# First chunks of the up projection through other banks and buffers, and the output projection queued one block later

## The chip, the cores and the metric

One core of a Trainium2 chip runs the whole program. The metric is the device time of one execution in microseconds (us), as the median of several runs. The engines are named as the profile names them: PE (matmuls and transposes), ACT (activations and copies), DVE (elementwise operations and scans), POOL, and SP, which here issues nearly all DMAs.

## The reference

One step of a decoder layer, in float32, for a prompt of 2048 tokens with 16 meta tokens ahead of it and for 8 decode sequences of one token each. What matters here, for the prompt:

```python
h = rmsnorm(xp, norm_mix_g)
q, k, v, u = project_mix(h, w_in)                 # 8 heads of 64, and 512 pooling channels
o_attn = stick_breaking(q, k, v, ...)             # blocks of 128 queries
o_pool = multiscale_pool(u, ...)
xp = xp + concat([o_attn, o_pool]) @ w_out        # 1024 x 1024
h2 = rmsnorm(xp, norm_ffn_g)
up = h2 @ w_up                                    # 1024 x 5632, causal conv of width 3, gate
xp = xp + (silu(gate) * val) @ w_down             # 2816 x 1024
y_prompt = rmsnorm(xp, norm_final_g)
```

`stick_breaking` gives each earlier key the weight sigmoid(z) times the product of (1 - sigmoid(z)) over the keys between it and the query. The decode tokens go through the same layer with cached keys and values of 4096 positions, read through a page table.

## The kernel before

All large matmuls are done in three passes (`mm3`, lines 156 to 161): both operands are split into a high and a low part (`split`, lines 152 to 154: a copy on ACT, then a subtraction on DVE), and high x high, high x low and low x high are added up in one PSUM bank.

The stages follow each other in the program text. Instructions are not issued in that order: a planner, run when the program is built, walks all instructions with estimated times and gives each engine its own fixed queue. Among instructions that it holds ready it takes the one that stands first in the text. On the chip each engine then works through its queue in order and waits on semaphores. So moving a call in the text changes its rank and with it the queues.

*Attention* (`attention`, lines 383 to 529) goes through four pairs of heads. For a pair, the units are a block `bi` of 128 queries (-1 is the meta tokens, then 0 to 15) by a chunk `c` of up to 512 keys. `chain` makes the scores `z` (line 450), two sigmoids on ACT, a scan along the keys on DVE (line 458) and a product on POOL or DVE (line 463). `weigh` follows three units later (LAG): transposes (line 493), copies, and products with the values into the bank `po` (line 508). After a block's last unit, `po` is copied to `ot`, stored to the DRAM tensor `cat_s` (line 517), and `done(bi)` is called.

For the last pair of heads `done` is `out_tile` (lines 573 to 593), the output projection of 128 rows. It loads those rows of `cat_s` into `cr` (line 578), splits them into `ch` and `cl`, does 48 matmuls into two `pso` banks (pool `ps_mm`), adds the residual (line 588), stores `xp_s`, normalises (`rstd_of`, line 592) and stores to `h2_s` (line 593). Row tile 1 + bi of `h2_s` is written by `out_tile(bi)`.

*Up projection* (lines 638 to 885). The 2048 rows are four chunks of 512 (`h2c[0]` to `h2c[3]`), held transposed and split, 32 KB per partition each. Iteration `it` takes the weights of one pair of 128-column slices (gate and value), and the two chunks of a half; each group is 24 matmuls into a `psu` bank. Ahead of the loop the first two chunks are made:

- Chunk 0 (lines 640 to 650): four loads of 128 rows (`xn0`, which shares the three `uwr` slots of the weights' pool `pu_w`), and for each load two groups of four transposes into a bank of `pu_mm` (six banks), each followed by `split`.
- The first weights, `load_up(0)` and `load_up(NF)` (line 671), through the same `uwr` slots.
- Chunk 1 by `h2_chunk(1)` (lines 655 to 669): two loads of 256 rows into slots of the decode's pool (`kvd`), and eight groups of transposes through the only bank of `pu_t`.

After that come the decode's preparations: `state_conv` through `kvd` slots and `pu_t` (lines 674 to 688), eight small loads of the page table `pt4` (lines 694 to 696), the index arithmetic on DVE (lines 699 to 703), and gathers of keys and values that run between the up projection's iterations.

Memory. The left pool of the attention stage (`pb`) and the right pool of the output projection (`pc`: its weights and rows) are closed before the up projection; the new pools lie over their bytes and banks, and a new tile waits for the old tiles that it covers (`reuse_waits="tile"`). The PSUM banks in order of the attention stage are: `ps_mm` 0 and 1, `ps_z` 2 and 3, `ps_t` 4 to 6, `ps_o` 7. The up projection's are `pu_q` 0, `pu_mm` 1 to 6, `pu_t` 7. In SBUF the new pools are stacked from where `pb` began: `pu_w` 36 KB, `h2a` 32 KB (chunk 0), `pu` 12 KB, `h2b` 2 x 32 KB (chunks 1 and 2), then the decode's pool.

Of the kernel before, what the change touches and what calls it, by code (L numbers as in the profile page):

```python
# [8 lines left out]
F32 = mybir.dt.float32  # L9
F32R = mybir.dt.float32r  # L10
# [5 lines left out]
PSUM = bass.MemoryType.PSUM  # L16
DRAM = bass.MemoryType.DRAM

P = 128
D = 1024  # L20
NK = D // P
# [9 lines left out]
NF = DFF // P  # L31
# [6 lines left out]
TILES = [(0, NS + META)] + [(NS + META + P * i, P) for i in range(SEQ // P)]  # L38
# [8 lines left out]
CW = 512  # L47
NCH = SEQ // CW
NSB = NS + 4
NSO = NS + 2  # L50
# [3 lines left out]
def f32(ap):  # L54
    return ap.bitcast(F32)
# [3 lines left out]
def hymba_kernel(  # L59
# [7 lines left out]
    nc = tc.nc  # L67
# [11 lines left out]
    def x_rows(dst, i):  # L79
        if i == 0:  # L80
            nc.sync.dma_start(out=dst[0:NS, :], in_=x_sample)
            nc.sync.dma_start(out=dst[NS:NS + META, :], in_=meta_tokens)
        else:
            return nc.sync.dma_start(out=dst, in_=x_prompt[P * (i - 1):P * i, :])
# [7 lines left out]
    h2_s = dram.tile([ACOLS, D], F32, name="h2_s")  # L92
# [6 lines left out]
    ident = con.tile([P, P], F32, name="ident")  # L99
# [26 lines left out]
    hsm = con.tile([P, NK, 32], F32, name="hsm")  # L126
# [3 lines left out]
    def rstd_of(pool, xt, n, sq=None):  # L130
        ss = pool.tile([P, 1], F32, name="ss")
        if sq is None:
            sq = pool.tile([P, D], BF16, name="sq", bufs=1)
        else:
            sq = pool.tile([P, D], BF16, name="sq", tag=sq[0], bufs=sq[1])
        nc.scalar.activation(out=sq[:n, :], in_=xt[:n, :], func=AF.Square, accum_out=ss[:n, :])
        ms = pool.tile([P, 1], F32, name="ms")
        nc.vector.tensor_scalar(out=ms[:n, :], in0=ss[:n, :], scalar1=1.0 / D, scalar2=EPS, op0=ALU.mult, op1=ALU.add)
        r = pool.tile([P, 1], F32, name="rr")
        t = pool.tile([P, 1], F32, name="rt")  # L140
        ri, ti = r.bitcast(I32), t.bitcast(I32)
        nc.vector.tensor_single_scalar(ti[:n, :], ms[:n, :].bitcast(I32), 1, op=ALU.logical_shift_right)
        nc.vector.tensor_scalar(out=ri[:n, :], in0=ti[:n, :], scalar1=-1.0, scalar2=float(0x5F3759DF),
                                op0=ALU.mult, op1=ALU.add)
        for _ in range(3):
            nc.vector.scalar_tensor_tensor(out=t[:n, :], in0=r[:n, :], scalar=r[:n, 0:1], in1=ms[:n, :],
                                           op0=ALU.mult, op1=ALU.mult)
            nc.vector.tensor_scalar(out=t[:n, :], in0=t[:n, :], scalar1=-0.5, scalar2=1.5, op0=ALU.mult, op1=ALU.add)  # L148
            nc.vector.tensor_tensor(out=r[:n, :], in0=r[:n, :], in1=t[:n, :], op=ALU.mult)
        return r  # L150

    def split(hi, lo, src):
        nc.scalar.copy(hi, src)  # L153
        nc.vector.tensor_tensor(out=lo, in0=src, in1=f32(hi), op=ALU.subtract)  # L154

    def mm3(ps, terms):
        n = len(terms)
        for i, (ah, al, bh, bl) in enumerate(terms):
            nc.tensor.matmul(ps, ah, bh, start=i == 0, stop=False)  # L159
            nc.tensor.matmul(ps, ah, bl, start=False, stop=False)  # L160
            nc.tensor.matmul(ps, al, bh, start=False, stop=i == n - 1)  # L161
# [5 lines left out]
    psm = main.enter_context(tc.tile_pool(name="ps_mm", bufs=2, space=PSUM, reuse_waits="tile"))  # L167
    psz = main.enter_context(tc.tile_pool(name="ps_z", bufs=2, space=PSUM, reuse_waits="tile"))
    pst = main.enter_context(tc.tile_pool(name="ps_t", bufs=3, space=PSUM, reuse_waits="tile"))
# [403 lines left out]
    def out_tile(bi):  # L573
        if bi < 0:
            return
        c0, n = TILES[bi + 1]
        cr = pc.tile([P, NK, P], F32, name="cr")
        nc.sync.dma_start(out=cr, in_=cat_s[:, :, c0:c0 + n].rearrange("c p n -> p c n"))
        ch = pc.tile([P, NK, P], F32R, name="ch", bufs=CHB)
        cl = pc.tile([P, NK, P], F32R, name="cl", bufs=CHB)  # L580
        split(ch, cl, cr)
        xt = pc.tile([P, D], F32, name="xt2", bufs=2)
        x_rows(xt, bi + 1)
        for hf in range(2):
            cs = slice(hf * 512, (hf + 1) * 512)
            ps = psm.tile([P, CW], F32, name="pso", tag="psm")
            mm3(ps, [(ch[:, c, :], cl[:, c, :], wo[c][0][:, cs], wo[c][1][:, cs]) for c in range(NK)])
            nc.vector.tensor_tensor(out=xt[:, cs], in0=ps, in1=xt[:, cs], op=ALU.add)
        nc.sync.dma_start(out=xp_s[c0:c0 + n, :], in_=xt)
        xn = pc.tile([P, D], F32, name="xn2")  # L590
        r = rstd_of(pc, xt, n, sq=("xn2", 1))
        nc.vector.scalar_tensor_tensor(out=xn, in0=xt, scalar=r[:, 0:1], in1=gffn, op0=ALU.mult, op1=ALU.mult)
        nc.sync.dma_start(out=h2_s[c0:c0 + n, :], in_=xn)

    attention(3, [], out_tile)
    main.close()


    puw = ctx.enter_context(tc.tile_pool(name="pu_w", bufs=3, reuse_waits="tile"))
    h2ctx = ctx.enter_context(ExitStack())  # L600
    pha = h2ctx.enter_context(tc.tile_pool(name="h2a", bufs=1, reuse_waits="tile"))
    h2c = {}

    def load_up(f):
        wr = puw.tile([P, NK, P], F32, name="uwr")
        nc.sync.dma_start(out=wr, in_=w_up[:, f * P:(f + 1) * P].rearrange("(c p) f -> p c f", p=P))
        wh = puw.tile([P, NK, P], F32R, name="uwh")
        wl = puw.tile([P, NK, P], F32R, name="uwl")
        split(wh, wl, wr)
        return wh, wl  # L610
# [12 lines left out]


    psq = ctx.enter_context(tc.tile_pool(name="pu_q", bufs=1, space=PSUM, reuse_waits="tile"))
    psm = ctx.enter_context(tc.tile_pool(name="pu_mm", bufs=6, space=PSUM, reuse_waits="tile"))
    pst = ctx.enter_context(tc.tile_pool(name="pu_t", bufs=1, space=PSUM, reuse_waits="tile"))
    HF = NF // 2

    def load_act(pool, hf, a0, n):  # L630
# [5 lines left out]
        return ah, al  # L636

    with ExitStack() as es:
        pu = es.enter_context(tc.tile_pool(name="pu", bufs=2, reuse_waits="tile"))
        h2c[0] = pha.tile([P, 2, NK, CW], F32R, name="h2c")  # L640
        for a in range(4):
            xn = puw.tile([P, NK, P], F32, name="xn0", tag="uwr").rearrange("p c n -> p (c n)")
            nc.sync.dma_start(out=xn, in_=h2_s[TILES[1 + a][0]:TILES[2 + a][0], :])
            for c4 in range(0, NK, 4):
                tp = psm.tile([P, 4, P], F32, name="tp0", tag="psu")
                for c in range(4):
                    nc.tensor.transpose(tp[:, c, :], xn[:, (c4 + c) * P:(c4 + c + 1) * P], ident)
                if a == 0:
                    nc.vector.tensor_copy(hsm[:, c4:c4 + 4, NSO:NSB], tp[:, :, 0:2])
                split(h2c[0][:, 0, c4:c4 + 4, a * P:(a + 1) * P], h2c[0][:, 1, c4:c4 + 4, a * P:(a + 1) * P], tp)  # L650
        phb = es.enter_context(tc.tile_pool(name="h2b", bufs=2, reuse_waits="tile"))
        dec = es.enter_context(ExitStack())
        dp = dec.enter_context(tc.tile_pool(name="dec", bufs=KVB, reuse_waits="tile"))

        def h2_chunk(ch):

            h2c[ch] = (pha if ch == 3 else phb).tile([P, 2, NK, CW], F32R, name="h2c")
            for a2 in range(0, 4, 2):
                c0 = TILES[1 + 4 * ch + a2][0]
                xn2 = dp.tile([P, 4, 512], F32, name="xn3", tag="kvd").rearrange("p k f -> p (k f)")  # L660
                nc.sync.dma_start(out=xn2.rearrange("p (a d) -> p a d", a=2),
                                  in_=h2_s[c0:c0 + 2 * P, :].rearrange("(a p) d -> p a d", p=P))
                for a in (a2, a2 + 1):
                    xn = xn2[:, (a - a2) * D:(a - a2 + 1) * D]
                    for c4 in range(0, NK, 4):
                        tp = pst.tile([P, 4, P], F32, name="tp3")
                        for c in range(4):
                            nc.tensor.transpose(tp[:, c, :], xn[:, (c4 + c) * P:(c4 + c + 1) * P], ident)
                        split(h2c[ch][:, 0, c4:c4 + 4, a * P:(a + 1) * P], h2c[ch][:, 1, c4:c4 + 4, a * P:(a + 1) * P], tp)

        ws_first = [load_up(0), load_up(NF)]
        h2_chunk(1)
        sc_v = state_conv.rearrange("b j f -> (b j) f")
        for f0 in range(0, 44, 11):
            room = dp.tile([P, 4, 512], F32, name="sc", tag="kvd").rearrange("p k f -> p (k f)")
# [18 lines left out]
        for b in range(NB):  # L694
            nc.sync.dma_start(out=pt4[:, b:b + 1],
                              in_=page_table[b, :].rearrange("(n o) -> n o", o=1).unsqueeze(1).broadcast_to([NPAGE, 4, 1]))
# [375 lines left out]
```

## Time and profile before

| | |
|---|---|
| median of 3 runs | 2898.42 us (2897.55 to 2900.72) |
| the profiled execution | 2897.86 us, its span 2895.9 us |
| PE busy | 2735.5 us, 94% of the span |
| DVE busy | 1822.0 us, 63% |
| ACT busy, POOL busy | 1040.0 us, 828.5 us |
| mean granted clock of PE | 0.971 |
| last products of attention | at 1204.1 us |

The profile is one execution, recorded by the hardware. The span runs from its first to its last instruction. "Busy" counts the time in which an engine has an instruction running; matmuls overlap each other, so a busy PE need not be at full speed, which is why the granted clock stands beside it. A wait is named by the instruction that waited and the one that ended the wait, with the engine, the tile and the line of the kernel. Lines of helpers (`split`: L153 and L154; `mm3`: L159 to L161) appear under every caller, so the tile tells which one it is: `pso` is the output projection, `psu` the up projection, `tp` the transposes.

### The profile page before, as it was taken

The page shows a single profiled execution, that of the slowest core. Times are in us where ns is not written, and L with a number is a line of the kernel's source. Part 1 is how long each engine was busy: PE and PEld are TensorE (multiplying, and loading weights), DVE is VectorE, ACT ScalarE, POOL GpSimd, SP SyncE. Part 2 cuts the span into 40 slices and gives each one's busy share as a digit, 9 for nine tenths or more (in the row PEclk, how much of TensorE's full clock was granted, in tenths as well). Part 3 has the DMA queues.
Part 4 walks back from the last instruction along what each step waited for, and adds up shares of the span by engine and source line. Part 5 has one row for each costly group of instructions (what it writes and reads, how often), then busy time and mean ns, then how long its engine had stood idle before and what let it go on. Part 6 is the DMA issues. An engine that isn't in the chain of part 4 may idle for free.

```text
span 2895.9 us, 39676 instructions
## 1 busy us (share of the span) xinstructions
PE 2735.5 (94%) x14622; PEld 2111.1 (73%) x14622; DVE 1822.0 (63%) x3101; ACT 1040.0 (36%) x1801; POOL 828.5 (29%) x995
## 2 busy tenths in 40 slices
PE   5899999999989999779999998999999989999998
PEld 4677777777777777658877776777777767777766
DVE  6556787787787777549977776677764451214433
ACT  3345665665665445322322222222222230002111
POOL 0023233333333223116555454445543200000000
PEclk9899999999998999989999999999999999999999
DMA  6674344333425332346576565546655375566452
GB/s 210 239 258 142 115 128 167 112 121 123 138 68 161 118 107 83 109 148 230 189 277 231 174 227 205 177 165 228 213 182 196 130 271 174 173 194 207 160 199 89
DMA packets 319191, 495.10 MB, mean 171 GB/s; under 512 B 24079, under 2 KB 227095, under 8 KB 302597
## 3 DMA queue, kind: packets, MB, share of 16 engines
q1 hardware_dynamic: 300565, 358.35, 37.7%
q0 software_dynamic: 18432, 134.23, 12.6%
q8 instruction: 115, 1.88, 0.3%
q14 instruction: 79, 0.65, 0.1%
HBM read 391.27 MB, written 101.64 MB: 170 GB/s over the span
## 4 chain that ended last, share of the span: by engine, by line
PE 73%; DVE 4%; DMA 3%; issue 3%; ACT 1%; POOL 0%; SPq 0%; POOLq 0%; DVEq 0%; ACTq 0%
PE psu L159 11%; PE psu L160 11%; PE psu L161 11%; PE psd L159 6%; PE psd L161 5%; PE psd L160 5%; PE po L508 3%; PE dav L790 2%; PE tt L493 2%; PE z L450 2%; PE pso L159 2%; PE pso L161 2%; PE pso L160 2%; DVE om L458 2%; PE psm L161 2%
## 5 line engine op out<-in xcount | busy, mean ns | idle before, releaser
L159 PE MATMUL psu<-h2c,uwh 128*128 128x512 f32 x1408 | 555.7, 396 | 4.2 <-ACT uwh L153 2.9
L160 PE MATMUL psu<-h2c,uwh 128*128 128x512 f32 x1408 | 552.4, 392 | 0.0
L161 PE MATMUL psu<-h2c,uwl 128*128 128x512 f32 x1408 | 551.0, 392 | 0.0
L458 DVE TENSOR_TENSOR_SCAN om<-om,zero 128x513 f32<-128x513 f32 (+5 forms) x360 | 380.6, 1063 | 103.7 <-ACT om L451 58.6
L463 POOL TENSOR_TENSOR be<-be,om 128x512 f32<-128x512 f32 (+3 forms) x176 | 190.0, 1080 | 538.4 <-DVE om L458 284.9
L870 DVE SCALAR_TENSOR_TENSOR cv<-psu,par,cv 128x511 f32<-128x511 f32 (+1 forms) x352 | 260.5, 742 | 128.4 <-ACT cv L867 127.5
L159 PEld LDWEIGHTS psu<-h2c,uwh 128*128 128x128 f32 x1408 | 265.7, 189 | 87.3 <-issue 16.6
L160 PEld LDWEIGHTS psu<-h2c,uwh 128*128 128x128 f32 x1408 | 265.6, 189 | 63.3 <-issue 9.7
L161 PEld LDWEIGHTS psu<-h2c,uwl 128*128 128x128 f32 x1408 | 265.3, 189 | 62.7 <-issue 7.5
L451 ACT ACTIVATE om<-z,nbias 128x512 f32<-128x512 f32 (+5 forms) x360 | 212.9, 593 | 217.1 <-PE z L450 164.6
L881 POOL TENSOR_TENSOR cv<-cv,cv 128x512 f32<-128x512 f32 x88 | 188.5, 2142 | 312.8 <-DVE cv L875 217.2
L1039 DVE TENSOR_TENSOR xt<-psd,xt 128x512 f32<-128x512 f32 x64 | 44.1, 691 | 306.8 <-PE psd L161 306.8
L867 ACT ACTIVATE cv<-psu,par 128x512 f32<-128x512 f32 x176 | 136.6, 777 | 263.5 <-PE psu L161 242.9
L159 PE MATMUL psm<-hk,wh 128*128 128x512 f32 x512 | 208.7, 413 | 5.6 <-ACT wh L153 3.1
L452 ACT ACTIVATE be<-z,bias 128x512 f32<-128x512 f32 (+5 forms) x360 | 210.9, 588 | 1.0 <-PE tpx L209 0.9
L154 DVE TENSOR_TENSOR uwl<-uwr,uwh 128x1024 fp32r<-128x1024 f32 x94 | 124.7, 1328 | 137.4 <-ACT uwh L153 133.4
L160 PE MATMUL psm<-hk,wh 128*128 128x512 f32 x512 | 209.8, 410 | 0.0
L161 PE MATMUL psm<-hk,wl 128*128 128x512 f32 x512 | 207.8, 406 | 0.5 <-DVE rt L148 0.3
L493 PE MATMUL tt<-ident,be 128*128 128x128 f32 x1088 | 178.8, 287 | 24.7 <-POOL om L445 16.5
L159 PE MATMUL psd<-wd,ah 128*128 128x512 f32 x512 | 202.1, 397 | 0.0
L160 PE MATMUL psd<-wd,ah 128*128 128x512 f32 x512 | 200.7, 392 | 0.6 <-DVE wd L154 0.5
L161 PE MATMUL psd<-wd,al 128*128 128x512 f32 x512 | 201.1, 393 | 0.0
(226 smaller groups left out, 4836.7 us busy)
## 6 DMA issues: line engine op xcount, KB each, us to landing
hk<-hs_s SPq DMA_DIRECT2D x96, 512.0 KB
uwr<-in_w_up_dram SPq DMA_DIRECT2D x88, 512.0 KB
act_s<-sg SPq DMA_DIRECT2D x88, 256.0 KB
ar<-act_s SPq DMA_DIRECT2D x32, 704.0 KB
raw<-in_w_up_dram SPq DMA_DIRECT2D x40, 512.0 KB
xt<-in_x_prompt_dram SPq DMA_DIRECT2D x32, 512.0 KB
hs_s<-hk SPq DMA_DIRECT2D x32, 512.0 KB
uwr<-in_w_down_dram SPq DMA_DIRECT2D x22, 512.0 KB
```

Source lines behind the costliest of these rows:

```text
L154: nc.vector.tensor_tensor(out=lo, in0=src, in1=f32(hi), op=ALU.subtract)
L159: nc.tensor.matmul(ps, ah, bh, start=i == 0, stop=False)
L160: nc.tensor.matmul(ps, ah, bl, start=False, stop=False)
L161: nc.tensor.matmul(ps, al, bh, start=False, stop=i == n - 1)
L451: nc.scalar.activation(out=om[:M, e, 0:n], in_=z[:M, :n], func=AF.Sigmoid, scale=-SCALE, bias=nbias[:M, h:h + 1])
L452: nc.scalar.activation(out=be[:M, e, 0:n], in_=z[:M, :n], func=AF.Sigmoid, scale=SCALE, bias=bias[:M, h:h + 1])
L458: nc.vector.tensor_tensor_scan(out=rv, data0=rv, data1=zero[:M, 0:1].broadcast_to([M, n + 1]), initial=1.0 if top else st["prev"][:M, e, 0 ...
L463: (nc.gpsimd if cnt["mul"] % 2 == 0 else nc.vector).tensor_tensor(out=be[:M, e, m0:n], in0=be[:M, e, m0:n], in1=om[:M, e, m0 + 1:n + 1], o ...
L493: nc.tensor.transpose(tt[:, a, e, :M], be[:M, e, lo_:lo_ + P], ident[:M, :M])
L867: nc.scalar.activation(out=t, in_=ps, func=AF.Identity, scale=cpar(2, fi), bias=cpar(3, fi))
L870: nc.vector.scalar_tensor_tensor(out=t[:, o:], in0=ps[:, 0:CW - o], scalar=cpar(d, fi), in1=t[:, o:], op0=ALU.mult, op1=ALU.add)
L881: nc.gpsimd.tensor_tensor(out=cv[1], in0=cv[0], in1=cv[1], op=ALU.mult)
```

## The change

- `out_tile` is no longer called for the block that has just ended. `out_later` keeps it and calls `out_tile` for the block before; the last one is called after attention.
- The pool `pu_t` is opened ahead of `pu_mm`, so that it gets bank 1 and `pu_mm` gets banks 2 to 7.
- The pool `h2b` is opened ahead of `pu`, so that its two buffers follow directly on `h2a`, and `pu` comes after them.
- Chunks 0 and 1 are both made by a new function, `h2_first`, which is chunk 0's former code: loads of 128 rows through the `uwr` slots, transposes into `pu_mm` banks. The first weights are requested between the two chunks. `h2_chunk` remains for chunks 2 and 3.

```diff
-    attention(3, [], out_tile)
+    late = []
+
+    def out_later(bi):
+        late.append(bi)
+        if len(late) > 1:
+            out_tile(late.pop(0))
+
+    attention(3, [], out_later)
+    out_tile(late.pop())
     main.close()
...
     psq = ctx.enter_context(tc.tile_pool(name="pu_q", bufs=1, space=PSUM, reuse_waits="tile"))
+    pst = ctx.enter_context(tc.tile_pool(name="pu_t", bufs=1, space=PSUM, reuse_waits="tile"))
     psm = ctx.enter_context(tc.tile_pool(name="pu_mm", bufs=6, space=PSUM, reuse_waits="tile"))
-    pst = ctx.enter_context(tc.tile_pool(name="pu_t", bufs=1, space=PSUM, reuse_waits="tile"))
...
     with ExitStack() as es:
+        phb = es.enter_context(tc.tile_pool(name="h2b", bufs=2, reuse_waits="tile"))
+
+        def h2_first(ch):
+
+            h2c[ch] = (phb if ch else pha).tile([P, 2, NK, CW], F32R, name="h2c")
+            for a in range(4):
+                i = 1 + 4 * ch + a
+                xn = puw.tile([P, NK, P], F32, name="xn0", tag="uwr").rearrange("p c n -> p (c n)")
+                nc.sync.dma_start(out=xn, in_=h2_s[TILES[i][0]:TILES[i][0] + P, :])
+                for c4 in range(0, NK, 4):
+                    tp = psm.tile([P, 4, P], F32, name="tp0", tag="psu")
+                    for c in range(4):
+                        nc.tensor.transpose(tp[:, c, :], xn[:, (c4 + c) * P:(c4 + c + 1) * P], ident)
+                    if i == 1:
+                        nc.vector.tensor_copy(hsm[:, c4:c4 + 4, NSO:NSB], tp[:, :, 0:2])
+                    split(h2c[ch][:, 0, c4:c4 + 4, a * P:(a + 1) * P], h2c[ch][:, 1, c4:c4 + 4, a * P:(a + 1) * P], tp)
+
+        h2_first(0)
+        ws_first = [load_up(0), load_up(NF)]
+        h2_first(1)
         pu = es.enter_context(tc.tile_pool(name="pu", bufs=2, reuse_waits="tile"))
-        h2c[0] = pha.tile([P, 2, NK, CW], F32R, name="h2c")
...
-        phb = es.enter_context(tc.tile_pool(name="h2b", bufs=2, reuse_waits="tile"))
...
-        ws_first = [load_up(0), load_up(NF)]
-        h2_chunk(1)
```

More of the change, by code (lines that the diff above doesn't have):

```diff
@@ L638, in hymba_kernel @@
     with ExitStack() as es:
-        pu = es.enter_context(tc.tile_pool(name="pu", bufs=2, reuse_waits="tile"))
-        h2c[0] = pha.tile([P, 2, NK, CW], F32R, name="h2c")
[L641 to L650, printed above, removed]
-        phb = es.enter_context(tc.tile_pool(name="h2b", bufs=2, reuse_waits="tile"))
+        phb = es.enter_context(tc.tile_pool(name="h2b", bufs=2, reuse_waits="tile"))
[15 more added lines that the diff above has]
+        h2_first(1)
+        pu = es.enter_context(tc.tile_pool(name="pu", bufs=2, reuse_waits="tile"))
         dec = es.enter_context(ExitStack())
```

## The prediction

> **What bounds the kernel now.** I read the page first: engines, slices, the chain that ended last.
>
> ```profile
> span 2895.9 us, 39676 instructions
> PE 2735.5 (94%) x14622; PEld 2111.1 (73%) x14622; DVE 1822.0 (63%) x3101; ACT 1040.0 (36%) x1801; POOL 828.5 (29%) x995
> ...
> PE   5899999999989999779999998999999989999998
> ...
> PE 73%; DVE 4%; DMA 3%; issue 3%; ACT 1%; POOL 0%; SPq 0%; POOLq 0%; DVEq 0%; ACTq 0%
> ```
>
> TensorE (PE) is the bound: 94% busy, 73% of the last chain. The kernel becomes shorter only where PE idles or runs at a low clock. Of the 40 slices (72.4 us each) the two sevens, the 17th and 18th, are 1158 to 1303 us: the passage from attention to the up projection. The table of stretches there:
>
> ```profile
> core 0: us, PE busy (x) PEld busy (x) DVE busy (x) ACT busy (x) POOL busy (x), PEclk, DMA share, GB/s
> 1204.60:1225.00 20.40, 12.72 (x48) 10.05 (x48) 4.86 (x10) 1.04 (x1) 0.00 (x0) 0.83 0.41 132
> 1225.00:1240.00 15.00, 9.93 (x48) 7.80 (x49) 11.54 (x27) 8.27 (x13) 0.00 (x0) 0.77 0.82 243
> 1240.00:1250.00 10.00, 8.27 (x39) 6.40 (x37) 5.01 (x10) 2.78 (x4) 0.00 (x0) 1.00 0.99 329
> 1250.00:1270.00 20.00, 6.22 (x25) 3.98 (x25) 4.92 (x17) 3.52 (x6) 2.53 (x2) 0.56 0.18 48
> 1270.00:1280.00 10.00, 10.00 (x40) 8.19 (x41) 1.34 (x2) 0.59 (x1) 0.00 (x0) 0.85 0.04 11
> sum 75.40, PE 47.14 PEld 36.43 DVE 27.67 ACT 16.20 POOL 2.53; mean PE 9.43 PEld 7.29 DVE 5.53 ACT 3.24 POOL 0.51
> ```
>
> PE is idle for 75.40 - 47.14 = 28.3 us, and its granted clock falls to 0.56. PE's waits from 1204 to 1280 us (line, what for: total, times, longest) name all of it; they sum to 28.2 us:
>
> ```profile
> PE tp L668 <- DVE h2c L154: 14.5, 6, 7.5
> PE pso L159 <- ACT ch L153: 7.0, 1, 7.0
> PE psu L159 <- ACT uwh L153: 2.9, 2, 2.4
> PE tp L647 <- DMA xn<-h_s: 2.0, 1, 2.0
> PE tp L647 <- DVE xt L588: 0.8, 1, 0.8
> PE psu L159 <- ACT h2c L153: 0.7, 1, 0.7
> PE tp L668 <- DMA xn<-h_s: 0.3, 1, 0.3
> ```
>
> The timeline shows how the 7.0 us arise:
>
> ```profile
> 1204.10 0.48 PE L508 MATMUL po<-atm,vtm 32*128 32x128 f32 x2
> ...
> 1204.94 0.32 SPq L517 DMA_DIRECT2D cat_s<-ot  x1
> 1206.56 0.37 SPq L578 DMA_DIRECT2D cr<-cat_s  x1
> ...
> 1211.63 0.80 PE L159 MATMUL pso<-woh,ch 128*128 128x512 f32 x1 [7.04 <-ACT ch L153]
> ```
>
> The last block's result goes to DRAM, comes back and is split, while PE has nothing: block 14's projection was already done, *ahead* of block 15's last products. Last, what work costs at full clock, and what it cost here:
>
> ```profile
> 1190.00:1201.00 11.00, 10.62 (x44) 8.56 (x44) 0.84 (x2) 0.95 0.01 1
> 1204.00:1225.00 21.00, 12.72 (x48) 10.05 (x48) 1.31 (x2) 0.84 0.40 128
> ```
> ```profile
> 1225.00:1240.00 15.00, 6.03 (x16) 4.34 (x17) 0.00 (x0) 0.00 (x0) 0.77 0.82 243
> ...
> 1270.00:1280.00 10.00, 9.81 (x36) 7.72 (x37) 0.00 (x0) 0.00 (x0) 0.85 0.04 11
> 1300.00:1400.00 100.00, 98.72 (x432) 80.49 (x431) 25.95 (x54) 13.96 (x18) 1.00 0.65 222
> ```
> ```profile
> 1225.00:1232.00 7.00, 3.90 (x32) 3.46 (x32) 4.93 (x10) 4.08 (x8) 1.00 0.81 254
> 1247.00:1280.00 33.00, 7.49 (x32) 4.92 (x32) 5.53 (x8) 4.69 (x8) 0.69 0.21 58
> ```
>
> The three fences are the matmuls of the output projection (pso), of the up projection (psu) and the transposes (tp), each by itself, with the same columns. A 128x512 matmul at full clock takes 98.72 / 432 = 0.2285 us, an output tile of 48 so 11.0 us. 32 transposes take 3.90 us at full clock.
>
> **The change, part by part.**
>
> *The output projection a block later.* Same instructions, each tile queued behind the next block's products. At the end two tiles (14 and 15) follow attention. Tile 14's 11.0 us now lie behind block 15's products and not ahead, so these end about 11.0 us sooner; then tile 14 runs while block 15 makes its 7.0 us round trip. The wait goes, since 11.0 is more than 7.0, and with it the slow clock behind it: 48 matmuls took 12.72 us against 11.0, 1.7 us. Gain 8.7. On SP the load of `cr` for tile 14 no longer stands close behind its own store, and `h2_s` is written a block later; its earliest reader of tiles 13 to 16 is chunk 3, half a stage away, so nobody waits.
>
> Inside attention I count nothing. PE idles there 314.00 - 289.17 = 24.8 us in all, and hardly ever for the projection's input:
>
> ```profile
> 890.00:1204.00 314.00, 289.17 (x1714) 227.24 (x1712) 224.17 (x420) 141.41 (x272) 78.76 (x135) 0.97 0.33 107
> ```
> ```profile
> PE tt L493 <- POOL om L445: 8.7, 6, 2.5
> ...
> PE pso L159 <- ACT ch L153: 1.0, 1, 1.0
> ```
>
> A tile that is always ready could fill the 8.7 us, or one more tile's 11.0 us could lie uncovered at the start. I take 0, between +8.7 and -11.0.
>
> *PSUM banks.* `pu_t` goes in front of `pu_mm`, so the first transposes get banks of `ps_z`, `ps_t` and `po`, free once attention is done, and no longer the bank that the last projection holds until L588. That is the 0.8 us. `pu_t` gets that bank; its first user, the `state_conv` transposes, comes later.
>
> *Chunk 1 through six banks and through the weights' buffers.* Now each of its eight groups goes through one bank: transpose, copy on ACT, subtract on DVE, next. That is 14.5 + 0.3 + 0.7 = 15.5 us of PE idle. With six banks the chain is pipelined as chunk 0's is, whose rows show no wait for DVE's split. The slow clock goes too: 7.49 - 3.90 = 3.6 us on the transposes, and 9.81 - 36 x 0.2285 = 1.6 us on the matmuls behind them. Gain 20.7. Its loads also leave their place behind the last `h2_s` store: `h2b` now lies wholly in attention's bytes (102 KB by the tile sizes; its first buffer ends at 36 + 32 + 32 = 100 KB, before at 112 KB).
>
> It pays with loads. All eight h2 tiles and the weights share three `uwr` slots, a slot is free only when PE has transposed it, and PE takes the transposes after both projections. One such load is in the trace, chunk 0's fourth:
>
> ```profile
> 1226.26 0.32 SPq L643 DMA_DIRECT2D xn<-h_s  x1
> ...
> 1230.02 1.06 PE L647 MATMUL tp<-ident,xn 128*128 128x128 f32 x8 [2.05 <-DMA xn<-h_s]
> ```
>
> From issue to use 3.76 us, 2.0 of them idle PE. Chunk 1 has four more of this kind: between 0 (up-projection matmuls of chunk 0 fill the time) and 4 x 2.0 = 8.0. I take 4.0, half, because PE has such matmuls from the first weights on, but its queue cannot step over a late transpose.
>
> *What stays.* Chunk 0's fourth load (2.0 us) and the first weights, which come through the same slots after it (2.9 us, and 6.03 - 16 x 0.2285 = 2.4 us of slow clock): 7.3 us, the lower bound if they vanish too. `pu` moves to bytes of the output weights, free when the last projection's matmuls end, before its first use. The decode's buffers lose two h2 tiles and can only start sooner.
>
> *Sum.* 8.7 + 0.8 + 20.7 - 4.0 = 26.2 us. Behind 1280 us PE is gapless for long (100.00 us of psu stretch above with 98.72 busy in it, the rest other matmuls), so an earlier start is carried to the end. The profiled execution took 2897.86 us: 2871.7. The median of the runs is 0.56 us higher, so 2872.
>
> One rule beside it. On the clock the row says: after 7.0 us of idle the 48 matmuls cost 1.7 us extra. The Trainium skill, "TensorE: Matmul & The Clock Gate", Part 1, says that an idle window of about 3.4 us halves the clock and about 3.4 us of work restores it, so 1.7 us per long gap; here the trace agrees. For chunk 1 it would give one such charge for its 7.5 us gap where the rows give 5.2 us; by the page the sum would be 22.7 and the time 2875.6. I keep the rows: the clock there stood at 0.56 over 20 us, several short bursts each not enough to raise it.
>
> **The rivals.**
>
> *Slower: the projection takes PE at each block's edge.* Now a tile waits out its round trip, and in these 7 us PE issues the next units' scores. A tile that is already there goes ahead of them with 11.0 us of matmuls, and DVE's scans, which need the scores, start late. For it: DVE has 224.17 us of scans and other work in those 314 us, so it cannot lose much before it is the bound. Against: three units are queued ahead (LAG), and there are as many tiles as before. With 15 edges it decides from 26.2 / 15 = 1.75 us each; at 3 us each it costs 45: 2897.9 - 26.2 + 45 = 2917.
>
> *The loads and the page table eat it.* One row of DVE speaks for it:
>
> ```profile
> DVE pt L700 <- DMA pt<-in_page_table_dram: 6.3, 1, 6.3
> ```
>
> DVE stood 6.3 us for the page table with splits behind it, which made the 7.5 us wait of PE. If that wait stays in front of a split that PE needs, and chunk 1's loads cost their full 8.0, the gain is 26.2 - 4.0 - 6.3 = 15.9: 2882. Against: with chunk 1 split early there are matmuls and six banks to live on. The Trainium skill, same page, "Architectural detail", calls VectorE's queue strictly first in, first out; by that rule this rival is open wherever the wait is placed.
>
> *The order does not come out as meant*: tile 14 still runs ahead of block 15's products, since both are ready when PE is free. Then the 8.7 us stay: gain 17.5, 2881.
>
> *More*: transposes slip in between the two projections, slots turn over early, and the 7.3 us and the 4.0 go as well: 37.5 us, 2861.
>
> **How the numbers follow.** Forecast (gain 20 to 32) 0.60; loads and page table 0.13; order not as meant 0.08; more 0.09; slower 0.10. A measurement of this kernel tells about 0.2% (5.8 us) from no change; the two small-gain cases can fall below that with 11 us lost in attention, for which I give 0.06 as "same". So faster 0.84, same 0.06, slower 0.10. The range runs from "more" (2861, to 2860) to the small gains with half a tile's 11.0 us lost in attention (2882 + 5.5 = 2888); the slower case is left out. The forecast's own range is 2866 to 2878.
>
> **What the changed profile would show.** Right: block 15's last products directly followed by 96 pso matmuls without a gap near 7 us; 64 transposes through the L647 line's successor and none of chunk 1 through `pu_t`, with no wait of theirs for DVE above 1 us; PE idle between the end of attention and steady psu about 12 us in place of 28. Wrong: PE idle in attention's 314 us well above 24.8; PE waits for `xn` loads adding to more than 8 us; the page table's wait followed by one of PE.

## The result, and the profile after

| | before | changed |
|---|---|---|
| median of 4 runs each, us | 2897.99 (2895.94 to 2900.72) | 2876.00 (2874.99 to 2877.32) |
| span of the profiled execution, us | 2895.9 | 2874.3 |

The ratio is 0.9924, with a 95% interval of 0.9907 to 0.9941: faster by 22 us, where 26 had been forecast (2872). The sum came out nearly right; its terms did not, as the rows show. One execution among all the runs below, of 3421.88 us (the kernel with chunk 1 in its own room), was in a slow state and is left out. The page of the changed kernel, span, engines and PE's slices:

```profile
span 2874.3 us, 39685 instructions
PE 2724.3 (95%) x14622; PEld 2106.8 (73%) x14622; DVE 1826.1 (64%) x3101; ACT 1041.3 (36%) x1801; POOL 825.5 (29%) x995
...
PE   5899999999998999799999998999999999999998
```

The two sevens became one, the 17th slice: the passage still idles, but less. PE's waits from 1170 to 1300 us (engine, tile and line that waited, what for: total, times, longest):

```profile
PE tp L659 <- DMA xn<-h_s: 8.3, 2, 6.4
PE pso L159 <- ACT ch L153: 7.4, 1, 7.4
PE tp L694 <- DMA sc<-in_state_conv_dram: 5.4, 1, 5.4
PE tp L659 <- DVE xn L592: 1.1, 1, 1.1
```

The 14.5 us wait for DVE's split through one bank is gone. The 7.0 us round trip of the last block is **not** gone: it is 7.4 us. And there are 14.8 us of new waits, 13.7 of them for loads. PE's timeline says why the round trip stayed:

```profile
1182.64 0.88 PE L508 MATMUL po<-at,vt 128*64 128x128 f32 x12
1183.45 0.48 PE L508 MATMUL po<-atm,vtm 32*128 32x128 f32 x2
1191.38 0.79 PE L159 MATMUL pso<-woh,ch 128*128 128x512 f32 x1 [7.45 <-ACT ch L153]
```

Between block 15's last products and the next `pso` matmul PE has nothing to do: tile 14's projection ran right *ahead* of these products. What was gained instead lies earlier: PE's waits inside attention, from 890 us to its end, where before 8.7 us were for POOL's `om`, 3.5 for DVE's `ot` and 1.0 for `ch`:

```profile
PE pso L159 <- ACT ch L153: 6.5, 5, 3.4
...
PE tt L493 <- POOL om L445: 0.3, 1, 0.3
```

To compare kernels I use three marks in each profile: the last `cat_s` store of block 3 (A), the end of the last `pso` matmul (B), and the virtual start of the up projection (C = 1300 minus the `psu` matmuls recorded before 1300 us times 0.2285). All in us:

| kernel | start to A | A to B: attention and projection | B to C: passage | C to end | span |
|---|---|---|---|---|---|
| before | 897.5 | 326.7 | 39.5 | 1632.2 | 2895.9 |
| changed | 893.3 | 311.8 | 31.1 | 1638.1 | 2874.3 |
| queue alone (first experiment) | 895.1 | 312.9 | 40.6 | 1631.6 | 2880.2 |
| passage alone (second) | 895.9 | 325.7 | 31.8 | 1629.0 | 2882.4 |

So 14.9 us came from attention and 8.4 from the passage. The first column wanders by some us from profile to profile (893.3 to 897.5). The last does not only wander: it holds a loss and a gain that nearly cancel. Between the 301st and the 1201st `psu` matmul, with the same work in it, the kernel before takes 219.8 us (queue alone: 220.0), the changed one 230.6 and the passage alone 226.5. Before has no wait of PE from 1284 to 1724 us; the changed kernel waits from 1256 to 1696 us for the decode's DVE work and for chunk 2's rows, 6.0 us in all, and its granted clock falls to 0.91 around the longer wait (1416 to 1456 us):

```profile
PE dav L804 <- DVE zdec L738: 3.6, 1, 3.6
PE tp L684 <- DMA xn<-h_s: 2.1, 1, 2.1
```

Against that, the down projection (first to last `psd` matmul) takes 549.6 us where it took 554.3. It takes 554.2 to 556.1 in the four kernels of this document with the old order of the pools, and 548.6 to 551.1 in the ten with the new one. Why the waits came, and why the down projection gained, stays open.

### The profile page after: what moved, and what is told of

Read it like the earlier page. It is cut to its first block, busy times and chain, and to the rows that moved or that the text cites. A ratio compares the mean times of both kernels' runs of the same rounds, so it can differ in the third digit from the quotient of the medians.

```text
span 2874.3 us, 39685 instructions
## 1 busy us (share of the span) xinstructions
PE 2724.3 (95%) x14622; PEld 2106.8 (73%) x14622; DVE 1826.1 (64%) x3101; ACT 1041.3 (36%) x1801; POOL 825.5 (29%) x995
## 3 DMA queue, kind: packets, MB, share of 16 engines
q0 software_dynamic: 18432, 134.23, 12.8%
## 4 chain that ended last, share of the span: by engine, by line
PE 60%; DVE 8%; DMA 4%; issue 3%; ACT 1%; POOL 0%; SPq 0%; ACTq 0%; DVEq 0%; POOLq 0%
PE psu L159 10%; PE psu L160 9%; PE psu L161 9%; PE psd L159 5%; PE psd L161 5%; PE psd L160 5%; PE dav L804 2%; PE po L508 2%; DVE kvd L736 1%; PE z L450 1%; PE pso L161 1%; PE pso L159 1%; PE pso L160 1%; PE tt L493 1%; DVE om L458 1%
## 5 line engine op out<-in xcount | busy, mean ns | idle before, releaser
L463 POOL TENSOR_TENSOR be<-be,om 128x512 f32<-128x512 f32 (+3 forms) x176 | 182.4, 1036 | 550.0 <-DVE om L458 310.5
L895 POOL TENSOR_TENSOR cv<-cv,cv 128x512 f32<-128x512 f32 x88 | 195.4, 2221 | 267.6 <-DVE cv L889 215.9
L153 ACT CAST uwh<-uwr 128x1024 fp32r<-128x1024 f32 x94 | 99.0, 1056 | 270.3 <-PE psu L160 258.2
```

The lines of the kernel that those rows point to most:

```text
L463: (nc.gpsimd if cnt["mul"] % 2 == 0 else nc.vector).tensor_tensor(out=be[:M, e, m0:n], in0=be[:M, e, m0:n], in1=om[:M, e, m0 + 1:n + 1], o ...
L895: nc.gpsimd.tensor_tensor(out=cv[1], in0=cv[0], in1=cv[1], op=ALU.mult)
```

## The experiments

Each kernel was run beside the kernel before on the same chip (its medians there: 2894.8 to 2896.9). Executions of one kernel differ by up to 14 us (the kernel before on one chip: 2888.3 to 2902.1), and each profile is one of them. Where the difference of two medians and that of their ratios, times 2898, disagree, both are given.

**Each half of the change by itself.**

```diff
 (before)
-    attention(3, [], out_tile)
+    late = []
+    def out_later(bi): ...
+    attention(3, [], out_later)
+    out_tile(late.pop())
```

> The later output projection alone; banks, bytes and chunk 1 as before. Theory A (the gain of the change sits inside attention: a tile that is always ready fills PE's gaps there; in the traces the stretch from the first blocks' store, 897.5 and 893.3 us, to attention's last products, 1204.1 and 1183.7 us, went from 307 to 290 us, with the same work in it): about 17 us below before, near 2881. Theory B (the forecast's split: the gain sits in the passage to the up projection, and the queue gives only the round trip, 8.7): near 2889. If the gain is in neither half alone: within 5 us of before.

Measured: 2882.18 us, ratio 0.9953 (0.9938 to 0.9968), 13.6 us, near what the first theory gave.

```diff
 (changed)
-    attention(3, [], out_later)
-    out_tile(late.pop())
+    attention(3, [], out_tile)
```

> Banks, bytes and chunk 1 as in the change, the output projection at its old place. Theory A: the passage gained next to nothing, because PE stands 8.3 us for h2 loads and 5.4 us for a state_conv load in place of the 14.5 us behind the single bank: 0 to 5 us below before, 2893 to 2898. Theory B: 17.5 us below, near 2880.

Measured: 2887.05 us, ratio 0.9972 (0.9961 to 0.9984), 8.1 us: more than the first theory gave and half of what the second gave. The halves add up: 13.6 + 8.1 = 21.7 against 22. (Both figures are the ratio applied to 2898.) The queue, forecast at 8.7, is worth 13.6 though it leaves the round trip in place; the banks, bytes and loads, forecast at 17.5, are worth 8.1. The new waits are there without the late queue too (8.6 us for rows and 6.5 for state rows in the second kernel).

**The order that the forecast assumed.** Tile 14 is issued behind block 15's last product (`last_mm` holds it):

```diff
 (changed)
-        if len(late) > 1:
+        if len(late) > 1 and bi < 15:
             out_tile(late.pop(0))
+        elif bi == 15:
+            with tc.issue_after(last_mm[0].ins):
+                out_tile(late.pop(0))
```

> The change, with projection tile 14 held in PE's queue behind block 15's last products, which is the order that the forecast assumed. Its 11.0 us then cover the 7.4 us round trip of block 15. Forecast's step: 7.4 + 1.7 = 9 us below the changed kernel's 2876, near 2867. Rival D (tile 14 had filled real gaps of attention's tail, which now stay open): the gain falls by what it had filled, up to 10 us, so 2867 to 2877.

Measured: 2866.51 us, ratio 0.9897 (0.9881 to 0.9913), 9.5 us below the changed kernel (7.8 by the ratios). The wait for `ch` at the end is gone from PE's list. So the total is near the 8.7 that were forecast for this order. But the places are not only the ones forecast: by the marks A to B is only 5.4 us shorter (306.4). Counted from A, block 15's products end 6.4 us sooner and not 11.0; PE's idle time before them grew by 1.6 us, as the rival had it in small, and the rest was not found. B to C is 2.2 longer (33.3), and from the 301st to the 1201st `psu` matmul it takes 223.2 us where the changed kernel takes 230.6.

**What bounds the passage.** PE's timeline of the changed kernel, and SP's queue beside it (start, duration, line, transfer):

```profile
1205.15 2.78 PE L659 MATMUL tp<-ident,xn 128*128 128x128 f32 x24
1214.36 1.94 PE L659 MATMUL tp<-ident,xn 128*128 128x128 f32 x8 [6.43 <-DMA xn<-h_s]
1217.44 1.94 PE L659 MATMUL tp<-ident,xn 128*128 128x128 f32 x8 [1.14 <-DVE xn L592]
1221.28 2.79 PE L659 MATMUL tp<-ident,xn 128*128 128x128 f32 x12 [1.91 <-DMA xn<-h_s]
1229.50 1.35 PE L694 MATMUL tp<-ident,sc 16*128 16x16 f32 x11 [5.42 <-DMA sc<-in_state_conv_dram]
1230.78 1.11 PE L659 MATMUL tp<-ident,xn 128*128 128x128 f32 x4
1231.54 0.78 PE L159 MATMUL psu<-h2c,uwh 128*128 128x512 f32 x1
```
```profile
1206.48 1.47 SPq L614 DMA_DIRECT2D uwr<-in_w_up_dram  x2
1208.05 8.60 SPq L655 DMA_DIRECT2D xn<-h_s  x4
1217.36 0.32 SPq L593 DMA_DIRECT2D h_s<-xn  x1
1219.41 4.23 SPq L614 DMA_DIRECT2D uwr<-in_w_up_dram  x2
1223.69 2.79 SPq L691 DMA_DIRECT2D sc<-in_state_conv_dram  x4
```

The first product of the up projection stands on PE behind *all* of chunk 1's transposes and the first of the state rows; every one of these needs a load that could go only when a slot, or the place in SP's queue, came free. The four loads of chunk 1, merged in one row above, went out at 1208.05, 1213.61, 1215.33 and 1216.33 us. The second and third take the slots of the first two weights and went out 0.02 and 0.03 us after DVE had split these weights (at 1213.59 and 1215.30); the second:

```profile
1212.36 1.23 DVE L154 TENSOR_TENSOR uwl<-uwr,uwh 128x1024 fp32r<-128x1024 f32 x1 [0.96 <-ACT uwh L153]
```
```profile
1213.61 0.34 SPq L655 DMA_DIRECT2D xn<-h_s  x1
```

The fourth went out 0.02 us after the transposes of the first. So in this kernel the turn through the three slots sets when these loads go. First, all products of the first weight pair with chunk 0 ahead of chunk 1:

```diff
 (changed)
         ws_first = [load_up(0), load_up(NF)]
-        h2_first(1)
...
             for k in (2 * half, 2 * half + 1):
+                if (it, k) == (0, 1):
+                    h2_first(1)
```

> The change, with chunk 1's loads and transposes written behind the up projection's first 48 matmuls (inside iteration 0, ahead of its second chunk). Theory A: the loads were dear because all of chunk 1's transposes stood ahead of those 48 matmuls in PE's queue; 48 x 0.2285 = 11.0 us of matmuls then run while the loads come in: 8 to 14 us below the changed kernel's 2876, near 2865. Rival C (the loads are bound by the transfers themselves, so PE waits the same time at another place): within 4 us of 2876.

Measured: 2871.80 us, ratio 0.9915 (0.9899 to 0.9932), 4.2 below the changed kernel (2.6 by the ratios, and the intervals overlap), nearer the rival's 4 at most than the first theory's 8 to 14. The 8.3 us went, but PE now waits 6.1 us for the first weights in one piece, four weight loads hold the slots, and the last two row loads go out from 1231.94 us on, behind the page table's.

Next, is it enough to take chunk 1 out of the shared slots? Chunk 1 gets the decode's `kvd` slots back, with the six banks kept:

```diff
 (changed)
-        h2_first(1)
...
-                        tp = pst.tile([P, 4, P], F32, name="tp3")
+                        tp = psm.tile([P, 4, P], F32, name="tp1", tag="psu") if ch == 1 else pst.tile(...)
...
+        h2_chunk(1)
```

> The change, but chunk 1's rows loaded as before, by two loads of 256 rows into the decode's slots, and transposed into pu_mm banks. Theory S (PE's 8.3 us for h2 loads come from the three uwr slots, through which chunk 1's four tiles wait behind chunk 0's transposes and the first weights): 5 to 9 us below the changed kernel's 2876, 2867 to 2871. Rival C (the transfers themselves and SP's queue bound it; the decode's slots are free only when the last projection's matmuls are done): within 4 us of 2876.

Measured: 2877.36 us, ratio 0.9945 (0.9932 to 0.9958), no better than the changed kernel. Other slots alone do not help: with their own room the two loads stand on SP behind the weights and behind the last `h2_s` store, which waits for DVE's normalisation, and PE waits in one piece:

```profile
PE tp L683 <- DMA xn<-h_s: 19.2, 1, 19.2
```

The six banks alone, put into the kernel before (the same `tp1` edit, nothing else), tell what the banks are worth:

> The kernel before with one edit: chunk 1's transposes use the six pu_mm banks; loads, bytes and queue as before. The forecast's step (the single bank costs 15.5 us of idle PE and 5.2 us of slow clock): 18 to 21 us below before, near 2877. Rival (behind the bank the next thing is late, the load of chunk 1 behind the last h2 store at 1240 us and DVE's 6.3 us for the page table): 5 to 10 us below, near 2889.

Measured: 2895.37 us, ratio 0.9999 (0.9988 to 1.0010): nothing, less than either side had expected. The 14.5 us for DVE became a wait for the loads, since chunk 1's transposes now came ahead of the first products in PE's queue:

```profile
PE tp L668 <- DMA xn<-h_s: 16.7, 2, 16.5
```

So the single bank had been covering a load that was nearly as late. In this profile the passage is 6.2 us shorter all the same (B to C 33.3), and the time is lost behind it: from the 301st to the 1201st `psu` matmul it takes 227.1 us, with 5.0 us of waits, where before took 219.8. The state rows' wait was tried by moving their block of code behind the first group of products (a function called at `(it, k) == (0, 1)`):

> The change, with the state_conv rows (four loads and 44 small transposes) written behind the first 48 up-projection matmuls. In the changed kernel PE stands 5.4 us for their load. If that wait is real cost: 4 to 6 us below 2876, near 2871. Rival (the wait only covers another one, for chunk 1's last transposes and the weights): within 3 us of 2876.

Measured: 2875.91 us, ratio 0.9940 (0.9927 to 0.9953), the same. The first product came 19.5 us after chunk 0's first transposes and not 26.4, but the wait for the rows was met later (`tp L695 <- DMA sc`, 4.6 us); where the remaining 2 us went was not found. Tile 14 behind, own room for chunk 1 and later state rows all together:

> Tile 14 held behind block 15's products, chunk 1 through the decode's slots, state_conv rows later, all on the change. If the three costs are separate: 2866.5 less 5 to 9 for the slots and 4 to 6 for the state rows, 2852 to 2858. If loads and state rows hide each other: 2860 to 2867.

Measured: 2872.63 us, ratio 0.9925 (0.9912 to 0.9938): 6 us *worse* than tile 14 behind alone (8 by the ratios) and outside both ranges. The late `kvd` load is there again:

```profile
PE tp L687 <- DMA xn<-h_s: 17.3, 1, 17.3
```

But B to C is no longer than with tile 14 alone (33.8 against 33.3 us), so this wait does not explain the 6 us; what does was not found.

Then the order of the loads, chunk 1's ahead of the first weights', on SP and so in the slots too:

```diff
 (changed)
-        ws_first = [load_up(0), load_up(NF)]
         h2_first(1)
+        ws_first = [load_up(0), load_up(NF)]
```

> The changed kernel with the loads and transposes of chunk 1 written ahead of the first two weight loads, nothing else. Theory Q (what bounds the passage is the loads' place in the sync engine's queue): the last loads of chunk 1 no longer stand behind two weight loads and the wait for the last row store, so TensorE's 8.3 us of waiting for them shrinks to 3 or less; the weights come later, which the 10 us of chunk 1's transposes and the wait for the state rows cover; 2870 to 2874 us. Theory S (the three shared slots bound it: a load can go only when a slot's transposes are done, and these stand behind the last tile on TensorE): the loads go out at the same instants as their slots come free, the wait stays at 6 to 9 us, and the first weights come later on top: 2875 to 2882 us.

Measured: 2874.48 us (2868.10 to 2876.34), ratio 0.9926 (0.9914 to 0.9938): at the upper end of what the first theory gave and inside what the second gave, so the total does not tell them apart. The rows, from the profile of an execution of 2868.82 us, say more:

```profile
PE tp L694 <- DMA sc<-in_state_conv_dram: 10.8, 1, 10.8
...
PE tp L659 <- DMA xn<-h_s: 3.0, 1, 3.0
```

The wait for rows fell from 8.3 to 3.0 us. That fits the first theory, but also the slots, since the rows now take theirs before the weights do; the edit moves both. And what the rows gained the state rows' wait lost (10.8 us for 5.4); the weights are late too: ACT starts to split them 0.9 us before that wait ends. Its timeline:

```profile
1225.14 1.04 ACT L153 CAST uwh<-uwr 128x1024 fp32r<-128x1024 f32 x1 [2.92 <-DMA uwr<-in_w_up_dram]
...
1228.91 0.78 PE L159 MATMUL psu<-h2c,uwh 128*128 128x512 f32 x1
```

Rows, weights and state rows come through one queue, and putting one ahead puts another behind. In this stretch the transfers themselves are dense too; in the changed kernel:

```profile
1210.00:1220.00 10.00, 3.88 (x16) 3.13 (x16) 7.98 (x16) 4.44 (x6) 0.00 (x0) 0.62 0.85 265
```

(us, busy time of PE, weight loads, DVE, ACT and POOL, then PE's clock, the DMA engines' busy share, GB/s): at a share of 0.85 the transfers may leave little to win by order alone; no run shows how little.

**Do the gains of the two places add?** Tile 14 behind, and chunk 1 behind the first 48 products:

> The changed kernel with both single edits that gained: tile 14 is issued behind block 15's last product (2866.5 alone) and chunk 1's passage behind the first 48 products of the up projection (2871.8 alone, 4.2 below the changed kernel). If the two gains lie in different places (the end of the attention and the start of the up projection), they add: 2876.0 - 9.5 - 4.2 = about 2862 us, 2859 to 2866. If the products that stand ahead of chunk 1 only fill the same empty time that tile 14 fills when it stands last, they do not add: 2866 to 2868. If tile 14's later stores of the normalised rows push the second chunk's loads back by their whole length on the sync engine's queue, worse than 2868.

Measured: 2860.57 us, ratio 0.9880 (0.9866 to 0.9894), 15.4 us below the changed kernel (12.8 by the ratios) where the two gains sum to 13.7 (10.4). They add.

**Why the late queue shortens attention.** The kernel before with the projection two blocks late and nothing else:

```diff
 (queue alone)
-        if len(late) > 1:
+        if len(late) > 2:
             out_tile(late.pop(0))
...
-    out_tile(late.pop())
+    while late:
+        out_tile(late.pop(0))
```

> The kernel before with the output projection alone queued two blocks late instead of one (tiles 14 and 15 both behind the attention). Theory G (what the queueing gained is that a ready tile stands beside every block and fills TensorE's gaps; one block of lateness is enough for that): the attention itself gains nothing more than one block late gave, about 15 us against before, and now tile 14 stands behind the last product and covers the wait for the last block's store and load, as the forecast had it for one block: 2882.2 - 9 = about 2873 us, 2870 to 2877. Rival (each block of lateness takes a further wait out of the attention): another 10 to 15 us beyond that, 2858 to 2864. Rival (tile 14 has no room: its products only lengthen the tail): 2881 to 2886.

Measured: 2854.73 us, ratio 0.9859 (0.9845 to 0.9874), 27 us below one block late: beyond even the rival's range. About 9 of them are the round trip and its slow clock, which tile 14 now covers. My theory that a ready tile had stood beside every block already fell. From the last `cat_s` store of block 3 to the last `pso` matmul, first the queue one block late, then two:

```profile
895.00:1207.80 312.80, 292.69 (x1736) 231.21 (x1735) 219.78 (x419) 136.66 (x261) 66.52 (x132) 0.97 0.34 109
```
```profile
897.10:1180.60 283.50, 282.69 (x1735) 227.37 (x1735) 217.92 (x418) 136.30 (x261) 69.85 (x132) 1.00 0.37 120
```

The same matmuls; two blocks late PE is busy for 282.69 of 283.50 us at a clock of 1.00, so 19 us of idle time, the round trip's among them, and the slow clock are gone. A likely reason shows in how long a tile's products stand behind the start of its split on ACT (tiles by counting 48 matmuls each in PE's order; us):

| | tile 6 | 8 | 10 | 12 | 14 |
|---|---|---|---|---|---|
| before | 8.4 | 5.4 | 6.6 | 1.3 | 1.1 |
| changed, one block late | 1.1 | 2.5 | 1.1 | 3.9 | 1.3 |
| two blocks late | 12.5 | 14.5 | 14.6 | 20.6 | 10.0 |

One block late in the program text, the planner still put most tiles' products close behind their split. Of the changed kernel, tile 14:

```profile
1158.06 0.32 SPq L517 DMA_DIRECT2D cat_s<-ot  x1
...
1159.66 0.37 SPq L578 DMA_DIRECT2D cr<-cat_s  x1
...
1165.04 1.08 ACT L153 CAST ch<-cr 128x1024 fp32r<-128x1024 f32 x1
...
1166.31 0.48 PE L159 MATMUL pso<-woh,ch 128*128 128x512 f32 x1
```

Any delay of store, load or split then stops PE: the 6.5 us in five waits shown above. Two blocks late, a whole block lies between, the tile can fill gaps of the block beside it, and no wait for `ch` is left in attention or behind it; PE's whole list from 890 to 1161 us:

```profile
PE tt L493 <- POOL be L463: 0.9, 1, 0.9
PE po L508 <- ACT om L451: 0.7, 1, 0.7
PE tt L493 <- DVE at L486: 0.4, 1, 0.4
PE z L450 <- ACT be L452: 0.3, 1, 0.3
```

The table does not explain the first step, from the kernel before to one block late. There the tiles stand on the whole no further behind their split than before, PE waits for `ch` more (6.5 us for 1.0), and yet the waits for POOL went and attention got shorter. That the change of queue did it is shown by the first experiment; how, stays open.

**All that gained, together:** the changed kernel, two blocks late, and chunk 1 behind the first 48 products.

> The changed kernel with the output projection queued two blocks late instead of one, and with chunk 1's passage behind the first 48 products of the up projection. Theory (the gains lie in three places and add): two blocks late gave 2854.7 with the passage of before; the changed passage by itself gave 8 to 10 us (2887.1 against 2895.4), and the 48 products ahead of chunk 1 another 4 to 6: 2854.7 - 8 - 5 = about 2842 us, 2837 to 2847. Rival (with two tiles left behind the attention, the passage's loads and weights have that time to come in anyway, so the changed passage hides nothing more): 2851 to 2856. Rival (the second of two late tiles stores its normalised rows so late that the second chunk's loads stand behind that store on the sync engine's queue): 2856 to 2865.

Measured: 2837.86 us (2837.38 to 2839.86), ratio 0.9804 (0.9791 to 0.9818): 57 us faster than before and 38 faster than the change (35 by the ratios). PE's waits from 893 to 1300 us sum to 10.1:

```profile
PE tp L660 <- DMA xn<-h_s: 4.9, 2, 3.5
PE z L450 <- ACT be L452: 1.6, 2, 1.2
PE psu L159 <- ACT uwh L153: 1.6, 1, 1.6
PE tp L694 <- issue: 1.5, 1, 1.5
PE pso L161 <- DVE cl L154: 0.5, 1, 0.5
```

By the marks: 285.9 us from A to B and 25.9 from B to C (326.7 and 39.5 before), 54.4 of the 58.5 us by which its span is shorter.

## Why the prediction was right or wrong

The time (2872 against 2876.0) and the sign were right, by errors that offset each other: that it came so close is luck.

*The output projection a block later: the step "tile 14's 11.0 us now lie behind block 15's products and not ahead" failed.* I took the order of the text for the order of the queue. The rival "order does not come out as meant" describes what happened; its time, 2881, missed for the next reason. Where the order is forced it is worth 9.5 us (7.8 by the ratios), near the 8.7, but in part at other places than the sum had them: 5.4 us from A to B, and much of the rest far behind.

*"Inside attention I count nothing" failed, and is the largest error.* The clause I set aside, that a ready tile could fill the 8.7 us behind POOL, came true (8.7 to 0.3), and 14.9 us were won there. PE's idle time fell by 9.8 of them (24.8 to 15.0); the rest fits the granted clock, 0.97 before and 0.99 after. Why the waits for POOL went is open, as said. Of the slower rival there is no sign: the stage got shorter. Together: forecast 8.7, measured 13.6 to 14.9.

*The bank of the first transposes* (0.8): that wait is gone. *Chunk 1 through six banks* (20.7, loads minus 4.0): the waits for DVE's split went, as forecast. But the loads were mis-sized. I charged them as more of the one 2.0 us row, up to 8.0; the new waits in the passage are 8.3 for chunk 1's rows, 1.1 in front of its transposes that the profile puts down to DVE's last normalisation, and 5.4 for the state rows, 14.8 us, where before 2.0 (chunk 0's fourth load) and 0.3 had been for rows. I had put "matmuls from the first weights on" between the transposes; in PE's queue there were none, since all 32 transposes of chunk 1 came first. And with a load that late the banks by themselves are worth nothing in time, and 6.2 us of the passage in one profile, as their experiment shows; my 20.7 priced a stall whose successor was already standing behind it. Net for the passage: 17.5 forecast, 8.1 to 8.4 measured.

*What stays* (7.3): it did not stay. The wait for the first weights, 2.9, went, covered by the new ones. So did chunk 0's fourth load: eight of its transposes slipped in between the projection's matmuls, as the rival "more" had it, and the 24 at 1205.15 us follow without a wait:

```profile
1193.25 1.91 PE L659 MATMUL tp<-ident,xn 128*128 128x128 f32 x8
1194.81 0.70 PE L161 MATMUL pso<-woh,cl 128*128 128x512 f32 x1
```

*Loads and page table* (2882): its half about the loads came true and beyond. The page table's did not; DVE's row there is now this, and no wait of PE follows from it:

```profile
DVE pt L714 <- DMA qb<-qd_s: 2.3, 1, 2.3
```

*"An earlier start is carried to the end"* held only in sum. The changed kernel lost 10.8 us between the 301st and the 1201st `psu` matmul, to 6.0 us of waits and the slow clock with them, which the row of before (98.72 us busy in 100) could not show, and won 4.7 in the down projection, which I had not counted.

*The sum:* 26.2 + (14.9 - 8.7) - (17.5 - 8.4) - 1.7 (first and last column of the table) = 21.6, the difference of the spans. Of the signs named as wrong, "waits for `xn` loads adding to more than 8 us" came (8.3), "idle in attention well above 24.8" did not (294.00 - 278.99 = 15.0). Of those named as right, chunk 1's transposes came through the other banks, with a wait of 1.1 us put down to DVE where 1 was the limit; the 96 `pso` matmuls without a gap did not come, and PE idles 22.2 us (7.4 + 8.3 + 5.4 + 1.1) and not 12 between the end of attention and the steady products. The row of attention:

```profile
890.00:1184.00 294.00, 278.99 (x1705) 220.28 (x1705) 217.54 (x408) 137.58 (x264) 66.65 (x133) 0.99 0.34 108
```

*The clock.* Behind the 7.45 us gap, the last 48 projection matmuls and these eight transposes took from 1191.38 to 1205.15 us, 13.8; at full clock they are 11.0 + 8 x 3.90 / 32 = 12.0. The gap cost 1.8 us besides itself, as before (1.7). The Trainium skill ("TensorE: Matmul & The Clock Gate", Part 1) gives about 3.4 us of sustained work until the clock is back at full speed; half of that, 1.7 us, is an estimate of the charge from the page's figure, and this trace agrees. For chunk 1 I had kept the rows against one such charge; the next section but one shows the rows of the changed passage, where one charge would again be too little. That the sum with the single charge (2875.6; rightly added, 2875.7) lies nearest to the result confirms nothing: both sums held the two steps that failed.

## What to carry to other kernels

The rank of a call in the program text is not its place in an engine's queue: before pricing a reordering, ask what the scheduler will do with it, and afterwards read how far each consumer stands behind its producer. Here one block later in the text left that distance at 1 to 4 us in the tiles shown, and only two blocks later brought it to 10 to 20 us; that step was worth another 27 us, some 9 of them for the round trip at the end. When a stall is to be removed, look for what the next instruction in the queue would wait for a moment later; a resource that costs 14.5 us in the list of waits can be worth nothing. Follow a gain to the end of the span: here 10 us of it were lost again behind the passage. Where several loads share slots and one issuing queue, moving one forward moves another back, and only work that needs none of them fills the gap.

## What the runs showed of the hardware

Short bursts of work between waits left TensorE's clock low. In the changed passage the 24 transposes at 1205.15 us took 2.78 us, 0.12 each. Behind the 6.43 us wait 8 took 1.94, 0.24 each; and the next bursts, behind waits of only 1.14 and 1.91 us, were no faster (8 in 1.94, 12 in 2.79; the rows stand with the passage above). Then came a wait of 5.42 us. The first products still started 0.43 us apart where 0.23 is full speed, up to 1235.96 us:

```profile
1232.12 0.63 PE L160 MATMUL psu<-h2c,uwh 128*128 128x512 f32 x1
1232.54 0.63 PE L161 MATMUL psu<-h2c,uwl 128*128 128x512 f32 x1
...
1236.56 0.39 PE L159 MATMUL psu<-h2c,uwh 128*128 128x512 f32 x1
```
```profile
1205.00:1236.00 31.00, 16.10 (x80) 13.66 (x79) 18.83 (x43) 11.79 (x19) 0.00 (x0) 0.62 0.69 195
```

So two waits over 5 us with two of 1 to 2 us between them went with half speed for 21.6 us (1214.36 to 1235.96). Of the 16.10 us in which PE was busy there, all but the first 2.78 were at about half speed; at full speed they would have been about 6.7 us shorter, an estimate from these rows. Set beside the 14.8 us of waits in this passage, that is nearly half as much again.
